# Gate over row sum moved from the attention probabilities to the transposed branch outputs of a hybrid decoder trunk

## The chip, the core and the metric

One core of a Trainium2 chip runs the whole program as one launch. TensorE (PE, with its weight loads as PEld), VectorE (DVE), ScalarE (ACT), GpSimd (POOL) and the queue that starts the DMAs (SP) each take their instructions in a fixed order; semaphores hold an instruction back until its inputs and its output buffer are there. The metric is the device time of the launch in microseconds (us): 1985.64 us before, the median of 3 runs (1984.42 to 1986.34).

## The reference

Two decoder layers on x of 512 tokens by 1024 channels, float32. Each normalises x, projects it, runs three token mixers, merges them by per-channel sigmoid gates, projects back, and ends with a SwiGLU block. The change lies in the mixers A (8 heads in 2 groups, head size 64) and B (8 heads):

```
p_c = masked_softmax(s_c, mask_c);  o_c = einsum(p_c, v_c)      # A: compressed blocks
p   = masked_softmax(s, ...);       o_s = einsum(p, vs)         # A: selected blocks
p_w = masked_softmax(s_w, mask_w);  o_w = einsum(p_w, vw)       # A: window
g   = sigmoid(gate_logits)                                      # per token, head and branch
o   = g[..., 0:1] * o_c + g[..., 1:2] * o_s + g[..., 2:3] * o_w
# B:  o = einsum(masked_softmax(q k), v), no gate
```

With 512 tokens there are 8 blocks and the top 16 of them are taken, and the window is 512 wide, so the selected and the window branch both attend to all earlier tokens, each with its own keys and values.

## The kernel before

Activations lie with channels on the 128 partitions and the 512 tokens along the row, except in the attention, where scores have 128 query tokens on the partitions. Float32 products are made of float32r parts: `split` writes hi = copy (ACT) and lo = source - hi (DVE or POOL), and `mm3` (lines 113 to 115) adds three products. Weights stream from memory, are split the same way (lines 100 and 101, tiles wr, wh, wl) and used by `gemm_gen`.

Attention is a pipeline over 24 jobs in each layer: 16 for mixer A (head h, branch b = 0 selected or 1 window, in the order h0b0, h0b1, h1b0, ...) and 8 for B. `attn` walks steps g; a job starts every 3 steps. In a step:

- `st_s`: score products into a PSUM tile of tag "s" (2 banks); DVE adds the mask and takes the row minimum (line 633); ACT takes the exponential into P0 to P3 and sums the row (line 636).
- `st_n`, at step 4 of the job: for A jobs DVE takes the reciprocal of the row sums (line 643) and multiplies each P by gate and reciprocal (line 645). For B jobs only the reciprocal is taken (line 647), once for a pair of heads.
- `st_t`, TLAG steps behind the scores: PE transposes P into a bank of tag "t" (3 banks, line 660); ACT and DVE split it into the float32r tiles pt or z.
- `st_v`, VLAG steps behind that: value products into the one bank "o" (lines 673 and 674). The two branches of an A head add up in one PSUM group. After the second, ACT and DVE join the hi and lo halves into half of a tile (lines 682, 683); after an odd head PE makes the compressed branch's product (line 688), DVE adds it (689), and the tile is split. For B, ACT spreads the reciprocals over a tile (692), PE transposes it (697), and DVE multiplies (698).

Between these, `fill` lets PE run weight products (the fillers: gates, B's projections, merges) by a rate worked out from due steps, and `step` runs background pieces (rope and norms of later heads, on POOL in this stage). The order within an engine is set when the program is built, by a scheduler that takes ready instructions in program order; weight loads and splits are moved up by 90 places. Tiles of a tag turn through a fixed number of buffers, and a new tile waits until the last reader of the old one is done.

## Time and profile before

| | us |
|---|---|
| median of 3 runs | 1985.64 |
| the profiled execution, its own time | 1982.81 |
| its span, first to last instruction | 1981.0 |
| attention of layer 0, about | 113 to 345 |
| attention of layer 1, about | 1088 to 1322 |

The profile is of one execution. "Busy" is the union of an engine's instructions; matmuls overlap in it, so the distance from one start to the next tells more of PE's pace than a duration. A wait is the idle time in front of an instruction, with the instruction that ended it. [...]

### The profile page before, as it was taken

The numbers are of one execution on the slowest core, as the hardware profiler recorded it, in microseconds if no ns is written. First come the engines' busy times: TensorE is split into PE (matmuls) and PEld (weight loads), VectorE is DVE, ScalarE is ACT, GpSimd is POOL, SyncE is SP. The second block draws the span as 40 slices with busy tenths as digits, with TensorE's granted clock in tenths as the row PEclk, the third lists the DMA queues.
The fourth block names the chain that finished last, engine by engine and source line by source line (L and its number), as shares of the span: only waits on it lengthen the run. The fifth ranks groups of instructions, "written<-read, shape, count | busy, mean of one in ns | idle before, by whom it ended". The sixth has DMA issues, their size and how long they took to land.

```text
span 1981.0 us, 26967 instructions
## 1 busy us (share of the span) xinstructions
PE 1935.6 (98%) x9472; PEld 1627.8 (82%) x9472; DVE 1319.7 (67%) x2783; ACT 996.6 (50%) x1937; POOL 252.0 (13%) x232
## 2 busy tenths in 40 slices
PE   9898999999999999999999899999999999999999
PEld 8777878888888888888888688888888888888887
DVE  8689998788545554455556999878874465534542
ACT  5466776687334332233344577857773343323331
POOL 0453442000000000000004536310000000000000
PEclk9999999999999999999999999999999999999999
DMA  5211101223333223323432111113233322333333
GB/s 159 86 56 34 41 31 43 87 94 104 109 125 101 96 96 93 99 98 96 131 112 93 43 41 44 38 46 100 95 102 119 121 91 100 96 94 99 97 102 100
DMA packets 100519, 173.94 MB, mean 88 GB/s; under 512 B 11936, under 2 KB 26144, under 8 KB 100384
## 3 DMA queue, kind: packets, MB, share of 16 engines
q1 hardware_dynamic: 100384, 172.22, 27.3%
q8 instruction: 74, 1.21, 0.2%
q14 instruction: 61, 0.50, 0.1%
HBM read 167.98 MB, written 4.19 MB: 87 GB/s over the span
## 4 chain that ended last, share of the span: by engine, by line
PE 78%; DVE 8%; ACT 2%; issue 1%; POOL 0%; ACTq 0%; DVEq 0%; POOLq 0%
PE pst L114 9%; PE pst L113 9%; PE pst L115 9%; PE psmm L113 8%; PE psmm L114 8%; PE psmm L115 8%; PE pss L114 7%; PE pss L113 7%; PE pss L115 7%; PE pst L660 1%; DVE P L645 1%; DVE pss L633 1%; PE pso L673 1%; PE pso L674 1%; ACT P L636 1%
## 5 line engine op out<-in xcount | busy, mean ns | idle before, releaser
L100 ACT ACTIVATE wh<-wr 128x512 fp32r<-128x512 f32 (+3 forms) x640 | 387.5, 608 | 698.4 <-PE pst L114 261.0
L101 DVE TENSOR_TENSOR wl<-wr,wh 128x512 fp32r<-128x512 f32 (+2 forms) x526 | 355.1, 676 | 247.5 <-ACT wh L100 242.4
L101 POOL TENSOR_TENSOR wl<-wr,wh 128x512 fp32r<-128x512 f32 (+2 forms) x114 | 138.8, 1224 | 951.8 <-ACT wh L100 935.8
L113 PE MATMUL psmm<-h,wh 128*128 128x512 f32 x600 | 237.2, 395 | 3.7 <-ACT wh L100 2.8
L115 PE MATMUL psmm<-h,wl 128*128 128x512 f32 x600 | 235.2, 392 | 0.6 <-POOL wl L101 0.6
L114 PE MATMUL psmm<-h,wh 128*128 128x512 f32 x600 | 235.0, 392 | 0.0
L113 PE MATMUL pst<-h,wh 128*128 128x512 f32 x512 | 199.8, 390 | 0.0
L114 PE MATMUL pst<-h,wh 128*128 128x512 f32 x512 | 199.3, 389 | 0.0
L115 PE MATMUL pst<-h,wl 128*128 128x512 f32 x512 | 199.3, 389 | 0.0
L113 PEld LDWEIGHTS psmm<-h,wh 128*128 128x128 f32 x600 | 112.9, 188 | 26.4 <-ACT wh L100 3.2
L113 PE MATMUL pss<-h,wh 128*128 128x512 f32 x344 | 134.2, 390 | 0.0
L115 PE MATMUL pss<-h,wl 128*128 128x512 f32 x344 | 133.9, 389 | 0.0
L114 PE MATMUL pss<-h,wh 128*128 128x512 f32 x344 | 133.9, 389 | 0.0
L115 PEld LDWEIGHTS psmm<-h,wl 128*128 128x128 f32 x600 | 112.9, 188 | 24.6 <-POOL wl L101 1.1
L114 PEld LDWEIGHTS psmm<-h,wh 128*128 128x128 f32 x600 | 112.9, 188 | 20.8
L636 ACT ACTIVATE P<-pss,nm 128x512 f32<-128x512 f32 x192 | 100.1, 525 | 55.4 <-DVE nm L633 32.3
L113 PEld LDWEIGHTS pst<-h,wh 128*128 128x128 f32 x512 | 96.1, 188 | 20.2 <-ACT e L984 0.4
L115 PEld LDWEIGHTS pst<-h,wl 128*128 128x128 f32 x512 | 96.1, 188 | 20.1
L114 PEld LDWEIGHTS pst<-h,wh 128*128 128x128 f32 x512 | 96.1, 188 | 19.8
L633 DVE CUSTOM_DVE_ANT_0 pss<-pss,mask 128x512 f32<-128x512 f32 x192 | 93.7, 489 | 7.2 <-PE pss L115 5.8
L660 PE MATMUL pst<-ident,P 128*128 128x128 f32 x480 | 76.6, 274 | 11.5 <-DVE P L645 5.3
L660 PEld LDWEIGHTS pst<-ident,P 128*128 128x128 f32 x480 | 58.2, 141 | 28.1 <-issue 17.8
(423 smaller groups left out, 4303.4 us busy)
## 6 DMA issues: line engine op xcount, KB each, us to landing
wr<-w SPq DMA_DIRECT2D x240, 256.0 KB, 2.6
wr<-wfm SPq DMA_DIRECT2D x188, 256.0 KB, 2.6
wr<-wpc SPq DMA_DIRECT2D x32, 256.0 KB, 2.6
wr<-wo SPq DMA_DIRECT2D x32, 256.0 KB, 2.6
wr<-wb SPq DMA_DIRECT2D x32, 192.0 KB, 2.4
wr<-w SPq DMA_DIRECT2D x32, 192.0 KB, 2.3
mg<-xT SPq DMA_DIRECT2D x16, 256.0 KB, 2.7
wr<-wpa SPq DMA_DIRECT2D x16, 256.0 KB, 2.6
```

Source lines behind the costliest of these rows:

```text
L100: self.A.activation(hi, src, AF.Copy)
L101: (eng or self.V).tensor_tensor(lo, src, hi.bitcast(F32), OP.subtract)
L113: mm(ps, a[0], b[0], start=first, stop=False)
L114: mm(ps, a[0], b[1], start=False, stop=False)
L115: mm(ps, a[1], b[0], start=False, stop=last)
L633: self.V.tensor_tensor_reduce(p[:, :W], p[:, :W], self.mask[:, 512 - W:], 1.0, 3e38, OP.add, OP.min, j.nm[:, i:i + 1])
L636: self.A.activation(j.Pi[i], p[:, :128 * (i + 1)], AF.Exp, bias=j.nm[:, i:i + 1], scale=-1.0, accum_out=j.l[:, i:i + 1])
L645: V.tensor_scalar(j.Pi[i], j.Pi[i], j.gate[:, i:i + 1], j.l[:, i:i + 1], op0=OP.mult, op1=OP.mult)
L660: self.T.transpose(ps[:, c:c + 128], j.Pi[i][:, kt * 128:kt * 128 + 128], self.ident)
L673: T.matmul(o[:, 512 - n:], j.V[kt], h[:, m0:m0 + n], start=j.first and kt == 0, stop=False)
L674: T.matmul(o[:, 512 - n:], j.V[kt], l_[:, m0:m0 + n], start=False, stop=j.last and kt == NT - 1)
```

## The change

The probabilities of mixer A stay unnormalised up to the value products. The sums of a pair of heads are kept per branch (tile lp0 or lp1), inverted and multiplied by the gates as a 128x8 tile, and spread by ACT over a 128x512 tile ("od") right away in `st_n` of the odd head; mixer B does the same without gate. Each branch gets its own group in bank "o", its own transposes of the spread tile (4 on PE) and its own multiplication on DVE; the branches are then added on POOL, and the compressed branch after that on DVE. Transposes go from 6 steps behind the scores to 4, value products from 2 behind them to 3. Tile pt gets 7 buffers, the zero-padded pair z is doubled and alternates by job, results get a tag "od" of 4 instead of "e" (3), and the scratch of software-made DMA descriptors is cut to 1024 bytes.

```diff
-TLAG, VLAG = 6, 2
+TLAG, VLAG = 4, 3
...
-        self.zp = [self.const([128, 512], f"z{j}", F32R) for j in range(2)]
+        self.zp = [[self.const([128, 512], f"z{j}{n}", F32R) for j in range(2)] for n in range(2)]
...
     def st_n(self, j, part):
         V = self.V
-        if j.cmp:
-            a = 2 - 2 * part
-            V.reciprocal(j.l[:, a:a + 2], j.l[:, a:a + 2])
-            for i in (a + 1, a):
-                V.tensor_scalar(j.Pi[i], j.Pi[i], j.gate[:, i:i + 1], j.l[:, i:i + 1], op0=OP.mult, op1=OP.mult)
-        elif j.h % 2 and part:
+        if j.h % 2 and part:
             V.reciprocal(j.lp, j.lp)
+            if j.cmp:
+                V.tensor_tensor(j.lp, j.lp, j.gate, OP.mult)
+            j.lb = self.pg("od")
+            self.A.activation(j.lb.rearrange("p (i h d) -> p i h d", i=NT, h=2),
+                              j.lp.rearrange("p h i -> p i h")[:, :, :, None].to_broadcast([128, NT, 2, 64]),
+                              AF.Copy)
...
     def st_v(self, j, s):
         T = self.T
-        if j.first and s == 0:
+        if s == 0:
             self.o = self.ps("o")
...
-            T.matmul(o[:, 512 - n:], j.V[kt], h[:, m0:m0 + n], start=j.first and kt == 0, stop=False)
-            T.matmul(o[:, 512 - n:], j.V[kt], l_[:, m0:m0 + n], start=False, stop=j.last and kt == NT - 1)
+            T.matmul(o[:, 512 - n:], j.V[kt], h[:, m0:m0 + n], start=kt == 0, stop=False)
+            T.matmul(o[:, 512 - n:], j.V[kt], l_[:, m0:m0 + n], start=False, stop=kt == NT - 1)
         if s < 2:
             return
...
+        odd = j.h % 2
+        if odd:
+            pc = self.ps("t")
+            for i in range(NT):
+                T.transpose(pc[:, i * 128:i * 128 + 128], j.lb[:, i * 128:i * 128 + 128], self.ident)
+        else:
+            self.od[j.b] = self.pg("od")
+        od = self.od[j.b]
+        r, s = (slice(64, 128), slice(0, 64)) if odd else (slice(0, 64), slice(64, 128))
+        self.A.activation(od[r], o[s], AF.Copy)
+        self.V.tensor_tensor(od[r], o[r], od[r], OP.add)
+        if not odd:
+            return
+        self.V.tensor_tensor(od, pc, od, OP.mult)
+        if j.cmp and j.b == 0:
+            return
+        if j.cmp:
+            o0 = self.od[0]
+            self.weng.tensor_tensor(od, od, o0, OP.add)
+            pc = self.ps("t")
+            r = slice((j.h // 2 % 2) * 64, (j.h // 2 % 2) * 64 + 64)
+            T.matmul(pc, self.vbd[j.h // 4][r], self.PcT[r], start=True, stop=True)
+            self.V.tensor_tensor(od, pc, od, OP.add)
...
+        self.split(hi, lo, od, self.weng)
+        self.yo.append((hi, lo))
```

What this does to the order, at three places of layer 0. First DVE where job h1b1 is normalised, before; bbcq and bbckv are the norm of B's compressed inputs, which run at the same time:

```order
L643 RECIPROCAL l_1611<-l_1611 128x2
L153 TENSOR_SCALAR bbckvi_1766<-bbckvv_1762 128x4
L154 TENSOR_SCALAR bbcqy_1743<-bbcqi_1745 128x4
L645 TENSOR_SCALAR P_1609<-P_1609,gth_830,l_1611 128x512
L157 TENSOR_TENSOR bbcqt_1744<-bbcqy_1743 128x4
L154 TENSOR_SCALAR bbckvy_1764<-bbckvi_1766 128x4
L645 TENSOR_SCALAR P_1608<-P_1608,gth_830,l_1611 128x384
L158 SCALAR_TENSOR_TENSOR bbcqt_1744<-bbcqt_1744,bbcqv_1741 128x4
L157 TENSOR_TENSOR bbckvt_1765<-bbckvy_1764 128x4
L643 RECIPROCAL l_1611<-l_1611 128x2
```

In these ten rows only the reciprocals and the products with P belong to the attention. The same place on DVE after (L640 and L642 are the reciprocal and the gate product, L631 the mask and minimum of line 633 before, which stands there as ISA):

```order
L640 RECIPROCAL lp_1379<-lp_1379 128x8
L642 TENSOR_TENSOR lp_1379<-lp_1379,gth_834 128x8
L631 ISA pss_1736,nm_1734<-pss_1736,mask 128x512
L631 ISA nm_1734 128x1
L686 TENSOR_TENSOR od_1706<-pso_1672,od_1706 64x512
L102 TENSOR_TENSOR z_103<-pst_1724,z_102 128x384
L320 TENSOR_SCALAR bbcqv_1747<-pst_1742 128x4
L320 TENSOR_SCALAR bbckvv_1768<-pst_1763 128x4
```

The four products over whole P tiles are gone; two 128x8 instructions stand in their place, and the norm of B comes behind minima and splits of the attention.

Second, PE at the end of the first pair of heads, before (L688 is the compressed branch, L660 the transposes of the next job):

```order
L674 MATMUL pso_1836<-z_103,v_847 128x256
L688 MATMUL pst_1980<-pct_1884,vbd_100 128x512
L660 MATMUL pst_1995<-ident,P_1716 128x128
L660 MATMUL pst_1995<-ident,P_1717 128x128
L660 MATMUL pst_1995<-ident,P_1718 128x128
L748 MATMUL pss_2001<-qk_1203,qk_1279 128x384
```

Here one bank of tag "t" is taken between the last value product and the next transposes. PE at the same place after (L680 transposes the spread tile, L697 is the compressed branch, L659 the transposes of P, L114 to L116 a filler):

```order
L673 MATMUL pso_1919<-z_105,v_851 128x256
L680 MATMUL pst_1958<-ident,od_1786 128x128 x4
L697 MATMUL pst_1967<-pct_1896,vbd_100 128x512
L659 MATMUL pst_1974<-ident,P_1733 128x128
L659 MATMUL pst_1974<-ident,P_1732 128x128
L659 MATMUL pst_1974<-ident,P_1733 128x128
L750 MATMUL pss_1985<-qk_1207,qk_1283 128x512
```

Four transposes have come in, and two banks of tag "t" in a row are taken by the end of the pair where one was.

Third, POOL around the addition of the branches (L694) of the third pair, after; L840 to L846 are the rope of B's queries, L102 the lo half of a split:

```order
L840 TENSOR_TENSOR e_3169<-big_2762,qn_1715 128x8x16
L694 TENSOR_TENSOR od_2793<-od_2793,od_2658 128x512
L844 TENSOR_TENSOR big_2761<-big_2761,qc_1714 128x8x32
L842 TENSOR_TENSOR e_3169<-big_2762,qn_1715 128x8x16
L846 TENSOR_TENSOR big_2761<-big_2761,e_3082 128x8x32
L844 TENSOR_TENSOR big_2762<-big_2762,qc_1714 128x8x32
L846 TENSOR_TENSOR big_2762<-big_2762,e_3169 128x8x32
```

L694 is new on POOL and stands among the rope of two tiles. Beside it DVE at the end of the first pair, after, where L698 adds the compressed branch to what L694 left:

```order
L686 TENSOR_TENSOR od_1706<-pso_1919,od_1706 64x512
L689 TENSOR_TENSOR od_1706<-pst_1958,od_1706 128x512
L631 ISA pss_1985,nm_1984<-pss_1985,mask 128x512
L631 ISA nm_1984 128x1
L698 TENSOR_TENSOR od_1706<-pst_1967,od_1706 128x512
```

One minimum stands between L698 and the product that L694 needs; before, the sum of the compressed branch (line 689) waited for no POOL work.

## Rows read from the trace of the kernel before

**Rows 1.** The page's first part: busy time, share, instructions.

```profile
PE 1935.6 (98%) x9472; PEld 1627.8 (82%) x9472; DVE 1319.7 (67%) x2783; ACT 996.6 (50%) x1937; POOL 252.0 (13%) x232
```

**Rows 2.** Windows over both attention stages and one stretch outside them.

```profile
core 0: us, PE busy (x) PEld busy (x) DVE busy (x) ACT busy (x) POOL busy (x), PEclk, DMA share, GB/s
113.00:150.00 37.00, 31.54 (x165) 24.78 (x163) 36.51 (x107) 20.91 (x52) 22.66 (x17) 1.00 0.16 49
150.00:190.00 40.00, 36.38 (x222) 31.37 (x222) 37.74 (x121) 26.23 (x76) 12.48 (x11) 0.96 0.08 26
190.00:230.00 40.00, 36.93 (x216) 32.09 (x217) 39.32 (x117) 29.34 (x73) 14.31 (x14) 1.00 0.11 32
230.00:270.00 40.00, 35.40 (x211) 29.87 (x210) 39.32 (x119) 29.40 (x78) 24.22 (x28) 1.00 0.17 54
...
345.00:640.00 295.00, 294.61 (x1300) 243.34 (x1299) 196.53 (x306) 166.12 (x256) 1.29 (x1) 1.00 0.32 104
1088.00:1130.00 42.00, 35.27 (x181) 27.30 (x181) 40.42 (x117) 23.81 (x58) 24.29 (x18) 0.99 0.17 55
1130.00:1170.00 40.00, 37.89 (x234) 33.13 (x235) 36.74 (x125) 27.79 (x79) 13.88 (x12) 0.97 0.10 31
1170.00:1220.00 50.00, 49.22 (x297) 44.19 (x296) 47.72 (x156) 40.98 (x104) 22.54 (x22) 1.00 0.14 40
1220.00:1270.00 50.00, 47.98 (x298) 40.37 (x297) 46.25 (x135) 37.70 (x104) 21.80 (x25) 1.00 0.13 41
```

**Rows 3.** Waits of PE, whole run: total us, times, longest us.

```profile
PE pss L748 <- ACT P L636: 10.6, 13, 1.4
PE pst L660 <- DVE P L645: 5.3, 3, 2.7
PE pst L660 <- DVE bbckvt L157: 4.4, 2, 2.9
PE pst L660 <- DVE l L643: 1.9, 1, 1.9
```

**Rows 4.** Groups of DVE, whole run: busy us, mean ns, idle before.

```profile
L645 DVE TENSOR_SCALAR P<-P,gth,l 128x512 f32<-128x512 f32 (+3 forms) x128 | 74.8, 609 | 0.4
...
L683 DVE TENSOR_TENSOR e<-pso,e 64x512 f32<-64x512 f32 x32 | 21.9, 685 | 5.7 <-ACT e L682 5.5
...
L643 DVE RECIPROCAL l<-l 128x2 f32<-128x2 f32 x64 | 9.2, 153 | 0.7 <-ACT P L636 0.7
```

**Rows 5.** Line 645 alone: duration min/median/max in ns, first and last start.

```profile
L645 DVE TENSOR_SCALAR P<-P,gth,l x128: 330/474/2056, 122.7 to 1244.8; 128x512 f32<-128x512 f32 x32, 128x384 f32<-128x384 f32 x32, 128x256 f32<-128x256 f32 x32, 128x128 f32<-128x128 f32 x32
```

**Rows 6.** Timeline of PE at a mixer B pair: start, us, what.

```profile
301.46 0.60 PE L697 MATMUL pst<-ident,e 128*128 128x128 f32 x4
301.90 0.60 PE L544 MATMUL pst<-ident,big 128*96 128x128 f32 x4
```

**Rows 7.** Timeline of PE at the end of a mixer A pair.

```profile
218.32 1.12 PE L688 MATMUL pst<-pct,vbd 64*128 64x512 f32 x2
219.38 0.55 PE L660 MATMUL pst<-ident,P 128*128 128x128 f32 x3
```

**Rows 8.** Timeline of PE behind its longest wait in layer 0's attention.

```profile
162.54 0.63 PE L660 MATMUL pst<-ident,P 128*128 128x128 f32 x4 [2.90 <-DVE bbckvt L157]
...
163.30 0.63 PE L114 MATMUL psmm<-h,wh 128*128 128x512 f32 x1
163.73 0.63 PE L115 MATMUL psmm<-h,wl 128*128 128x512 f32 x1
```

**Rows 9.** A group of ACT: the spread tile of mixer B.

```profile
L692 ACT ACTIVATE e<-lp 128x512 f32<-128x512 f32 x8 | 5.0, 629 | 0.0
```

**Rows 10.** Groups of POOL in layer 0's attention, 113 to 345 us.

```profile
L101 POOL TENSOR_TENSOR wl<-wr,wh 128x512 fp32r<-128x512 f32 x24 | 31.4, 1308 | 66.7 <-ACT wh L100 58.8 <-PE psmm L114 5.2 <-ACT e L576 2.7
...
L101 POOL TENSOR_TENSOR oT<-e,oT 128x512 fp32r<-128x512 f32 x4 | 5.1, 1283 | 9.2 <-ACT oT L100 9.2
```

More of the change, by code (lines that the diff above doesn't have):

```diff
@@ L93, in small @@
     def small(self, shape, tag, dt=F32):
-        return self.sm.tile(shape, dt, tag=tag, name=self.nm(tag), bufs=2 if tag in ("vec", "nm", "l", "lp") else 1)
+        return self.sm.tile(shape, dt, tag=tag, name=self.nm(tag), bufs=2 if tag in ("vec", "nm", "lp0", "lp1") else 1)
     def const(self, shape, name, dt=F32):
@@ L182, in consts @@
         self.vbd = [self.const([128, 128], f"vbd{g}") for g in range(2)]
-        self.zp = [self.const([128, 512], f"z{j}", F32R) for j in range(2)]
-        for t in self.kbd + self.vbd + [z[:, :128].bitcast(F32) for z in self.zp]:
+        self.zp = [[self.const([128, 512], f"z{j}{n}", F32R) for j in range(2)] for n in range(2)]
+        for t in self.kbd + self.vbd + [z[:, :128].bitcast(F32) for p in self.zp for z in p]:
             V.memset(t, 0.0)
@@ L654, in st_t @@
         else:
-            h, l_ = self.zp
+            h, l_ = self.zp[j.n % 2]
         ps = self.ps("t")
@@ L672, in st_v @@
             h, l_, m0, n = j.dst[kt]
-            T.matmul(o[:, 512 - n:], j.V[kt], h[:, m0:m0 + n], start=j.first and kt == 0, stop=False)
-            T.matmul(o[:, 512 - n:], j.V[kt], l_[:, m0:m0 + n], start=False, stop=j.last and kt == NT - 1)
+            T.matmul(o[:, 512 - n:], j.V[kt], h[:, m0:m0 + n], start=kt == 0, stop=False)
+            T.matmul(o[:, 512 - n:], j.V[kt], l_[:, m0:m0 + n], start=False, stop=kt == NT - 1)
         if s < 2:
             return
-        if j.last:
-            odd = j.h % 2
-            if not odd:
-                self.od = self.pg("e")
-            r, s = (slice(64, 128), slice(0, 64)) if odd else (slice(0, 64), slice(64, 128))
-            self.A.activation(self.od[r], o[s], AF.Copy)
-            self.V.tensor_tensor(self.od[r], o[r], self.od[r], OP.add)
-            if odd:
-                if j.cmp:
-                    pc = self.ps("t")
-                    r = slice((j.h // 2 % 2) * 64, (j.h // 2 % 2) * 64 + 64)
-                    T.matmul(pc, self.vbd[j.h // 4][r], self.PcT[r], start=True, stop=True)
-                    self.V.tensor_tensor(self.od, pc, self.od, OP.add)
-                else:
-                    lb = self.pg("e")
-                    self.A.activation(lb.rearrange("p (i h d) -> p i h d", i=NT, h=2),
-                                      j.lp.rearrange("p h i -> p i h")[:, :, :, None].to_broadcast([128, NT, 2, 64]),
-                                      AF.Copy)
-                    pc = self.ps("t")
-                    for i in range(NT):
-                        T.transpose(pc[:, i * 128:i * 128 + 128], lb[:, i * 128:i * 128 + 128], self.ident)
-                    self.V.tensor_tensor(self.od, pc, self.od, OP.mult)
-                if j.cmp:
-                    hi, lo = self.pg("oT", F32R), self.pg("oT", F32R)
-                else:
-                    hi, lo = self.pg("cq", F32R), self.pg("cq", F32R)
-                self.split(hi, lo, self.od, self.weng)
-                self.yo.append((hi, lo))
@@ L706, in attn @@
+        self.split(hi, lo, od, self.weng)
+        self.yo.append((hi, lo))
     def attn(self, jobs, hooks):
         n = 3 * len(jobs)
+        for i, j in enumerate(jobs):
+            j.n = i
         for g in range(n + TLAG + VLAG):
@@ L738, in a_jobs @@
                 j = Job()
-                j.h, j.first, j.last, j.cmp = h, b == 0, b == 1, True
+                j.h, j.b, j.cmp = h, b, True
                 def op(j=j, h=h, b=b):
@@ L918, in b_jobs @@
             j = Job()
-            j.h, j.first, j.last, j.cmp, j.gate = h, True, True, False, None
+            j.h, j.b, j.cmp = h, 0, False
             j.open = lambda: None
```

22 lines of the change are left out of this document (12 added, 10 removed).

## Prediction

> **What bounds the kernel now.** I read the page's first part, then windows, then PE's waits, then the groups of the engine that PE waits for, then PE's timeline. PE is busy for 98% of the span [rows 1], so time can only come from its few idle stretches or from work given to it. The windows say where those are: in 345 to 640 PE idles 0.39 of 295 us, while in the four windows that hold layer 0's mixer A jobs (113 to 270) length less busy time is 5.46 + 3.62 + 3.07 + 4.60 = 16.75 us, and in layer 1's (1088 to 1270) 6.73 + 2.11 + 0.78 + 2.02 = 11.64 us [rows 2]. Together 28.4 of 339 us. In layer 0's windows DVE is busy 36.51 + 37.74 + 39.32 + 39.32 = 152.9 of 157 us, or 97%; ACT 105.9, POOL 73.7 [rows 2]. So this stage has two nearly full engines, and PE waits for DVE: 11.6 us in transposes of P (5.3 + 4.4 + 1.9), and 10.6 us in score products that wait for a bank which ACT has to read, behind DVE's minimum [rows 3]. The 4.4 us have the name of B's norm, yet transposes of P need nothing of that norm; they need line 645, whose instructions stand between the norm's in DVE's order. All 11.6 us are thus waits for the normalisation.
>
> **What is removed.** 128 products over P, 74.8 us, and 64 reciprocals, 9.2 us [rows 4]: 84.0 us of DVE, 42.0 in each layer. These products last 330 to 2056 ns with a median of 474 [rows 5], so some are held up far beyond their length. [...]
>
> **What is added, by engine.**
> PE: 16 groups of four transposes (4 pairs, 2 branches, 2 layers). At a pair of mixer B the same four take 301.90 - 301.46 = 0.44 us from start to start [rows 6]; 16 x 0.44 = **+7.0 us**. Nothing hides this, since PE is the engine that the rest waits for in the end.
> DVE, a layer: 8 more joins of hi and lo at 685 ns, 5.5 us; 8 products from PSUM over 512 columns, taken at the same 685 ns, 5.5 us [rows 4]; 16 instructions of 128x8, bounded by 153 ns [rows 4] and by the 2056 ns of rows 5, taken at 0.2 us, 3.2 us. In all 14.2, so DVE loses 42.0 - 14.2 = 27.8 us a layer, and has 152.9 - 27.8 = 125 us of work left in a stage whose PE work is 140.2 + 3.5 = 143.7 us: 87%.
> ACT, a layer: 8 spread tiles at 629 ns [rows 9] and 8 copies out of "o", taken at as much: 10.1 us, so 116 of 144 us. POOL: 4 additions, as long as a 128x512 split, 1283 ns [rows 10]: 5.1 us. Neither becomes the fullest engine.
> At no cost: the second z pair and the two further pt buffers (memory alone), and the smaller scratch, since all loads are issued from SP. The lag of 4 would put transposes next to exponentials; but the scores of the next job's second step, right behind them in PE's order, wait for the same exponential's bank already, so a wait is brought forward by four transposes, not made. At most 0.44 us at each of the 13 waits of rows 3, 5.7 us; I take 0 and keep 5.7 for the range.
>
> **What PE gets back.** How much idle time is left at a DVE load of 87%? The trace has two windows of the same stage with a load under 97% and all kinds of jobs: 1170 to 1220 (DVE 95%, PE idle 0.78 of 50) and 1220 to 1270 (92%, 2.02 of 50) [rows 2]: 2.8% of the time. On 310.6 + 7.0 us of PE work that is 9.1 us. Line 645 first runs at 122.7 us [rows 5], so what PE waits before cannot change: a quarter of the 37 us window, and of the idle 5.46 and 6.73 us of the two first windows, 3.0 us. Left are 12.1 of 28.4: **-16.3 us**. From the other side: the 11.6 us for normalisation go, and half of the 10.6, which is 16.9. Bounds: 0 (each wait finds another releaser) and -28.4.
> [...] The granted share is 0.96 over 40 us there, and 0.99 over 42 and 0.97 over 40 us in layer 1 behind the wait of 2.7 us [rows 2, 3]: 1.6 + 0.4 + 1.2 = 3.2 us lost. Both waits are waits for line 645, so **-3.2 us**; bounds 0 and -3.2.
>
> **What is late next.** The end of a pair. Its transposes and the compressed product take two "t" banks in a row. The first is free after a copy (0.63), a join and a product (0.685 each), 2.0 us; until PE claims it again there are the compressed product, 219.38 - 218.32 = 1.06 us [rows 7], three transposes, two scores and, in most pairs, six filler matmuls: about 1.06 + 0.33 + 0.45 + 1.36 = 3.2 us, in the third pair 1.8 without the filler. The second bank is free only after the POOL addition (1.28) and line 698 (0.69), 4.0 us, and is wanted about 5 us on. DVE stands still in line 698 until POOL is done; behind it stand the z split, for which value products wait, and minima, for which ACT's exponentials and so the scores wait. On POOL the addition waits for DVE's product, with weight splits for the fillers behind it; on ACT the spread waits for two 128x8 instructions of DVE, with exponentials behind it, one for every second job. So with POOL free there is no wait, and 1 us to spare. POOL is not always free: in the third pair the addition stands amid B's rope. I take 1 us for each of the two third pairs and 0.15 for the other six: **+3.0 us**. Bounds: 0; and, if at each of 8 pairs POOL's row stands behind a weight split that waits 58.8 / 24 = 2.45 us for ACT [rows 10], 1.5 us beyond the spare time, 12 us, with 5 us more for each third pair, 22 us.
>
> **Sum.** +7.0 - 16.3 - 3.2 + 3.0 = -9.5 us. From the profiled execution, 1982.8 us (its span of 1981.0 and 1.8 around it), that gives 1973.3; that execution was 2.8 us under the median of the runs, so the forecast for the median is 1985.6 - 9.5 = **1976 us**.
>
> **Rivals.**
> The waits only move. For it: the chain from score to minimum to exponential stays, with two "s" banks, and the window 1220 to 1270 idles 4% though DVE has 8% of it free [rows 2]. Against: the 11.6 us hang on an instruction that is gone. Half the return: -8.1 - 1.6 + 7.0 + 3.0 = 0.3, **1986 us**, no change.
> The end of the pair becomes the bound: line 698 holds DVE until POOL comes, at every pair. New waits of 22 instead of 3 us make it -9.5 + 19 = +9.5, **1995 us**, slower. It decides from 12.5 us in all, 1.6 us a pair. For it: POOL's idle time is waiting for ACT with the queue shut behind it [rows 10]. Against: the order was made with L694 among instructions that are ready then, and POOL has 83 of 157 us free in layer 0.
> The stage becomes as dense as the rest: 0.1% idle [rows 2] beside the 3.0 us before the first normalisation, so -25.1 - 3.2 + 7.0 = -21.3 and **1964 us**. Against it is that no window of the attention under DVE's full load shows that.
> The transposes lower the clock. Each of the 16 new groups that brought half speed for as long as the long wait did would cost 1.6 us, 26 us in all: **2002 us**. Against: ten transposes of P a job and a granted share of 1.00 in five of the eight windows [rows 2]; it fell behind long waits alone [rows 8]. [...] No row shows a clock that fell among transposes without a wait ahead of it.
> That the change does not do what it says is hardly open: the order shows the removed and the added rows.
>
> **How the numbers follow.** Forecast 0.64, waits only move 0.16, end of the pair 0.10, dense stage 0.08, clock 0.02. The forecast's own range is 1969 to 1983: its return may be 5 us more or less, and the new waits 0 to 8. The range for 8 in 10 reaches to the rivals on both sides, 1965 to 1988: under it lies half of the dense case (0.04), above it the pair end, the clock and the worse end of waits that move (0.14). A change under 0.2% (4 us) cannot be told from none. Under 1981.7: 0.61 of the forecast's 0.64, and 0.08: 0.69. Above 1989.6: 0.10 + 0.02 and 0.02 of the moved waits: 0.14. Between: 0.17.
>
> **What would show it.** Line 660's waits for DVE should fall from 11.6 to under 2 us, the waits of scores for ACT from 10.6 to about 5; DVE busy in the stage's windows near 87%, their PE idle near 12 us in all, the clock 1.00; 96 transposes of spread tiles at 0.11 us apart; the attention stages shorter and 345 to 640 of the same length. Wrong would be: waits of transposes or of line 697 for DVE behind line 698 of 1.6 us or more at most pairs, waits of transposes for ACT, or a granted share under 0.95 in these windows.

## The result and the profile after

The changed kernel is slower: 2001.41 us median (four runs, 1998.42 to 2005.43) against 1985.66 us for the kernel before on the same chip, a ratio of 1.0081 with the interval [1.0062, 1.0101]. That is +15.8 us where -9.5 were forecast, and outside the range of 1965 to 1988 us. The profiled execution took 2002.57 us, 19.8 above the profiled one of before; that is 4 us more than the medians differ by, since the profiled one of before lies 2.8 us under its median and this one 1.2 above its own.

The first part of the page, kernel after, answers to [rows 1]:

```profile
PE 1952.0 (98%) x9536; PEld 1640.3 (82%) x9536; DVE 1289.7 (64%) x2657; ACT 1020.9 (51%) x1971; POOL 257.8 (13%) x240
```

Windows of the kernel before over its two attention stages, from the first score of a layer to its last value product (columns as in [rows 2]; the last of them but two, PEclk, is the granted share of TensorE's clock):

```profile
113.10:344.60 231.50, 213.37 (x1276) 182.45 (x1275) 217.12 (x628) 161.52 (x423) 92.21 (x85) 0.99 0.12 37
1088.70:1322.20 233.50, 221.53 (x1318) 189.72 (x1318) 213.22 (x634) 166.36 (x430) 97.78 (x89) 0.99 0.13 41
```

The same two stages of the kernel after, and six of the shorter windows that answer to [rows 2]:

```profile
113.90:352.10 238.20, 220.90 (x1308) 187.47 (x1307) 195.54 (x564) 172.18 (x439) 96.17 (x89) 0.98 0.11 36
1095.80:1342.30 246.50, 229.47 (x1350) 195.27 (x1350) 201.90 (x570) 176.66 (x446) 101.16 (x93) 0.98 0.12 39
...
113.00:150.00 37.00, 32.05 (x171) 26.06 (x170) 33.35 (x103) 23.11 (x58) 23.77 (x20) 0.96 0.14 45
150.00:190.00 40.00, 38.89 (x238) 33.99 (x238) 30.47 (x105) 28.85 (x79) 10.84 (x9) 0.95 0.10 32
190.00:230.00 40.00, 37.04 (x217) 31.15 (x216) 35.21 (x92) 30.69 (x75) 15.28 (x15) 1.00 0.10 32
230.00:270.00 40.00, 35.51 (x208) 30.24 (x207) 30.53 (x95) 29.77 (x76) 26.45 (x30) 0.96 0.17 53
...
1099.00:1140.00 41.00, 35.98 (x196) 29.54 (x195) 37.25 (x106) 22.02 (x54) 28.16 (x23) 0.96 0.13 43
1140.00:1180.00 40.00, 37.50 (x215) 31.90 (x216) 30.11 (x102) 30.35 (x83) 7.88 (x7) 0.91 0.09 28
```

Nearly all of the 19.8 us lies in the attention: 465.0 us before, 484.7 after, and what is outside them is 1516.0 and 1516.1 us. DVE did get free, 152.9 us before [rows 2] and 129.6 of 157 us now (33.35 + 30.47 + 35.21 + 30.53), 83%. PE did not use it. In the two stages PE idles 484.7 - 450.4 = 34.3 us, against 465.0 - 434.9 = 30.1 before, and it is busy for 15.5 us more, of which the 64 transposes explain 7.0. The granted share fell from 0.99 to 0.98; 0.95 and 0.96 stand in three of layer 0's four windows, where before there was one, and 0.96 and 0.91 in two of layer 1. Length times lost share, as the prediction took it, is 1.5 + 2.0 + 1.6 + 1.6 + 3.6 = 10.3 us in these five windows, against 3.2 before; an estimate, since the shares are rounded. By it about 7 us of the added busy time are work at the lower clock level (0.43 us from one 512-column product to the next in place of 0.23, as the pieces at the end of this document show), more than the 4.2 us of added idle time.

Waits of PE, kernel after (engine, line, what it waited for, total us, times, longest), answer to [rows 3]:

```profile
PE pss L114 <- ACT qk L101: 6.7, 10, 1.4
PE pss L750 <- ACT P L634: 6.1, 8, 1.4
PE pso L672 <- DVE od L686: 5.9, 6, 2.1
PE pst L659 <- ACT pct L615: 4.9, 2, 3.3
```

The 11.6 us behind line 645 are gone and scores wait 6.1 in place of 10.6 us, both as forecast. But the transposes of P (line 659) still wait 10.0 us in all, now for ACT's copy of the compressed probabilities ("pct", 4.9), for line 689 (2.3), for exponentials (2.2) and for B's norm (0.6). Other new waits stand beside them, and their names are those of the change: "od" is a head's output on its way out of the one "o" bank, and "qk" is a tile of mixer B that ACT splits in the step in which it now also copies such an output. Two views show this. First two of the lines that write "od", kernel after (count, duration min/median/max in ns; below, what DVE sat idle for ahead of such lines):

```profile
L686 DVE TENSOR_TENSOR od<-pso,od x48: 673/689/695, 145.6 to 1343.0; 64x512 f32<-64x512 f32 x48
L694 POOL TENSOR_TENSOR od<-od,od x8: 1280/1290/1292, 174.3 to 1275.8; 128x512 f32<-128x512 f32 x8
...
  ACT od L685: 14.0, 16
  POOL od L694: 6.9, 5
```

The durations are those that the prediction took (685 and 1283 ns). What it did not price is that DVE stands still 14.0 us for the copy, against 5.5 before [rows 4]; the 6.9 us that it stands still for POOL were to cost 3.0 with all else at the end of a pair. Then the timeline of ACT and of PE in layer 0's mixer B, kernel after (start us, us, engine, what, and in brackets the idle time before and its releaser):

```profile
296.28 0.59 ACT L685 ACTIVATE od<-pso 64x512 f32<-64x512 f32 x1
296.90 0.59 ACT L101 ACTIVATE qk<-pst 96x512 fp32r<-96x512 f32 x1
...
297.55 0.50 PE L114 MATMUL pss<-qk,qk 96*128 96x512 f32 x1 [1.30 <-ACT qk L101]
```

The copy of a head's output stands right ahead of the qk split in ACT's order, and PE waits 1.30 us for the split.

### The profile page after: what moved, and what is told of

It reads as the page before. It is cut to its first block, busy times and chain, and to the rows that moved or that the text cites. A ratio compares the mean times of both kernels' runs of the same rounds, so it can differ in the third digit from the quotient of the medians.

```text
span 2000.8 us, 26987 instructions
## 1 busy us (share of the span) xinstructions
PE 1952.0 (98%) x9536; PEld 1640.3 (82%) x9536; DVE 1289.7 (64%) x2657; ACT 1020.9 (51%) x1971; POOL 257.8 (13%) x240
## 4 chain that ended last, share of the span: by engine, by line
PE 79%; DVE 11%; ACT 6%; issue 2%; POOL 2%; DMA 0%; SPq 0%; ACTq 0%; DVEq 0%; POOLq 0%
PE pst L115 10%; PE pst L114 10%; PE pst L116 10%; PE psmm L116 8%; PE psmm L114 8%; PE psmm L115 8%; PE pss L114 7%; PE pss L115 7%; PE pss L116 7%; ACT P L634 1%; PE pst L659 1%; DVE pss L631 1%; DVE qk L551 1%; PE pso L672 1%; DVE pt L102 1%
## 5 line engine op out<-in xcount | busy, mean ns | idle before, releaser
L102 DVE TENSOR_TENSOR wl<-wr,wh 128x512 fp32r<-128x512 f32 (+2 forms) x526 | 352.0, 670 | 250.1 <-ACT wh L101 245.3
L102 POOL TENSOR_TENSOR wl<-wr,wh 128x512 fp32r<-128x512 f32 (+2 forms) x114 | 136.9, 1207 | 936.5 <-DVE wl L102 680.9
L114 PE MATMUL psmm<-h,wh 128*128 128x512 f32 x600 | 237.8, 396 | 5.1 <-ACT wh L101 4.4
L116 PE MATMUL psmm<-h,wl 128*128 128x512 f32 x600 | 236.7, 395 | 0.6 <-POOL wl L102 0.6
L114 PE MATMUL pst<-h,wh 128*128 128x512 f32 x512 | 199.6, 390 | 0.0
L116 PE MATMUL pst<-h,wl 128*128 128x512 f32 x512 | 199.2, 389 | 0.0
L114 PEld LDWEIGHTS psmm<-h,wh 128*128 128x128 f32 x600 | 113.9, 190 | 27.5 <-ACT wh L101 4.8
L116 PEld LDWEIGHTS psmm<-h,wl 128*128 128x128 f32 x600 | 113.8, 190 | 25.0 <-POOL wl L102 1.1
L114 PE MATMUL pss<-h,wh 128*128 128x512 f32 x344 | 134.1, 390 | 0.0
L116 PE MATMUL pss<-h,wl 128*128 128x512 f32 x344 | 133.9, 389 | 0.0
L116 PEld LDWEIGHTS pst<-h,wl 128*128 128x128 f32 x512 | 96.1, 188 | 20.1
L115 PEld LDWEIGHTS pst<-h,wh 128*128 128x128 f32 x512 | 96.1, 188 | 19.8
L114 PEld LDWEIGHTS pst<-h,wh 128*128 128x128 f32 x512 | 96.1, 188 | 19.8
L631 DVE CUSTOM_DVE_ANT_0 pss<-pss,mask 128x512 f32<-128x512 f32 x192 | 94.4, 492 | 17.4 <-PE pss L116 11.6
L659 PE MATMUL pst<-ident,P 128*128 128x128 f32 x480 | 78.4, 279 | 10.0 <-ACT pct L615 4.9
L659 PEld LDWEIGHTS pst<-ident,P 128*128 128x128 f32 x480 | 58.8, 143 | 28.3 <-ACT pct L615 5.6
```

Source lines behind the costliest of these rows:

```text
L102: (eng or self.V).tensor_tensor(lo, src, hi.bitcast(F32), OP.subtract)
L114: mm(ps, a[0], b[0], start=first, stop=False)
L115: mm(ps, a[0], b[1], start=False, stop=False)
L116: mm(ps, a[1], b[0], start=False, stop=last)
L631: self.V.tensor_tensor_reduce(p[:, :W], p[:, :W], self.mask[:, 512 - W:], 1.0, 3e38, OP.add, OP.min, j.nm[:, i:i + 1])
L659: self.T.transpose(ps[:, c:c + 128], j.Pi[i][:, kt * 128:kt * 128 + 128], self.ident)
```

## The experiments

Each time is a median beside the kernel before on the same chip (1984.75 to 1986.13 us); "difference" is against that one. Lags are written as transposes behind scores, values behind transposes; "place" is their sum modulo the three steps of a job, that is, in which of them a head ends. The ratio goes by all runs and the difference by medians; e15, where the two disagree in sign, shows no difference.

| run | edit | us | ratio [95%] | difference |
|---|---|---|---|---|
| e1 | after, lags 6, 2 | 1992.62 | 1.0043 [1.0030, 1.0056] | +7.9 |
| e2 | before, lags 4, 3 | 2008.56 | 1.0112 [1.0096, 1.0127] | +23.8 |
| e3 | before, no normalisation | 1967.19 | 0.9914 [0.9902, 0.9927] | -17.6 |
| e4 | after, no spread | 1992.72 | 1.0041 [1.0029, 1.0054] | +8.0 |
| e5 | e3 at lags 4, 3, with the z pairs and pt buffers of after | 1973.42 | 0.9948 [0.9934, 0.9962] | -12.0 |
| e6 | e4 at lags 6, 2 | 1988.42 | 1.0020 [1.0011, 1.0029] | +3.0 |
| e7 | after, lags 5, 2 | 2000.76 | 1.0080 [1.0067, 1.0092] | +15.3 |
| e8 | after, lags 5, 3 | 1987.48 | 1.0011 [1.0003, 1.0020] | +2.0 |
| e9 | after, L694 on DVE | 1994.91 | 1.0059 [1.0046, 1.0072] | +9.5 |
| e10 | e8, L694 on DVE | 1977.52 | 0.9960 [0.9948, 0.9972] | -7.9 |
| e11 | before, 2 of 4 products on ACT | 1981.53 | 0.9981 [0.9973, 0.9990] | -3.9 |
| e12 | before, all products on ACT | 1976.41 | 0.9953 [0.9941, 0.9965] | -9.0 |
| e13 | after, a head's end one step later | 2006.06 | 1.0105 [1.0092, 1.0118] | +20.7 |
| e14 | e10, no spread | 1974.13 | 0.9941 [0.9929, 0.9954] | -11.2 |
| e15 | e10, a head's end behind the scores | 1984.46 | 1.0004 [0.9994, 1.0014] | -0.9 |
| e16 | after, values and end behind the scores | 1994.44 | 1.0040 [1.0026, 1.0053] | +8.3 |
| e17 | e10 at lags 6, 3 | 1998.97 | 1.0067 [1.0054, 1.0080] | +12.8 |

**The four parts of the change, taken apart (e1 to e4).** The theory behind them: relief of DVE pays as forecast, and either the new lags or the new ends of the heads spend it.

```diff
 e1  -TLAG, VLAG = 4, 3          (in after)
     +TLAG, VLAG = 6, 2
 e2  -TLAG, VLAG = 6, 2          (in before; with the z pairs, pt buffers and scratch of after)
     +TLAG, VLAG = 4, 3
 e3  -            V.reciprocal(j.l[:, a:a + 2], ...)        (in before)
     -            for i in (a + 1, a):
     -                V.tensor_scalar(j.Pi[i], ...)
 e4  -        if odd:                                       (in after)
     +        if odd and not j.cmp:      # no transposes of a spread tile for A, no spread on ACT, no product
```

> The changed kernel with the old lags of 6 and 2. Theory 1 (the shorter way from scores to transposes and value products is what costs: waits for the bank of the value products, for the bank behind the compressed branch and for B's queries and keys are of order and latency, not of DVE load): back by 10 us or more, to 1985 to 1992, with the half-rate clock stretches of the attention down from 20.5 us to about 7. Theory 2 (the new form of the pair ends, 64 transposes and a bank per branch, costs by itself): 1997 to 2002 as the changed kernel.

> The kernel before with lags 4 and 3, 7 pt buffers, two z pairs and the small scratch, but the old normalisation of P by DVE. Theory 1 (the lags cost): slower than before by 10 us or more, since line 645 then stands straight in front of the transposes: 1996 to 2010. Theory 2 (the new pair ends cost): within 5 us of 1985.7.

> The kernel before without reciprocal and product over P for mixer A, nothing put in their place (the normalisation and the gates of mixer A are left out). It prices what DVE's relief alone is worth. If PE waits because DVE is full, as the prediction had it: 16 to 20 us less, 1966 to 1970. If the waits are of latency and only find another releaser: 0 to 8 us less, 1978 to 1986.

> The changed kernel without the spread tiles of mixer A, their 64 transposes and the products with them (mixer A stays unnormalised and without the gates of two branches); lags, banks and additions as changed. If the added PE work is the cost: 7 us less and the clock as it is, 1993 to 1995. If the two banks taken in a row at the pair ends, with the waits behind them, cost too: 10 to 15 us less, 1986 to 1991. If the lags cost: no more than 7 us less.

e3 settles the return. Its two stages:

```profile
114.30:337.20 222.90, 212.31 (x1276) 183.68 (x1275) 182.76 (x532) 161.52 (x423) 90.68 (x85) 0.98 0.13 39
1081.30:1306.50 225.20, 219.01 (x1318) 189.31 (x1318) 187.21 (x538) 166.46 (x430) 96.26 (x89) 1.00 0.14 43
```

PE has the same 1276 and 1318 instructions as before and idles 16.8 us in place of 30.1: 13.3 us from idle time, and 17.6 in the medians. So most of the prediction's return (16.3 and 3.2) is there when nothing is added. The clock's part of it is not seen: the share in e3's two stages is 0.98 and 1.00, where it was 0.99 in both. The two lags are then far from free: from e1 to the changed kernel they cost 2001.41 - 1992.62 = 8.8 us, and 23.8 on the old form. That e2 is so much worse has a reason of its own, in the waits of its profiled execution (2000.97 us, the fastest of its five):

```profile
PE pst L660 <- DVE P L645: 17.2, 14, 3.1
```

At a lag of 4 the transposes stand in the step of the normalisation that they need; the new form has no such line, so e2 says little of the change, and e5 was run for it.

**The lags on a relieved DVE, the groups without a spread, and two pairs of lags that tell distance from place (e5 to e8).**

```diff
 e5  e3 with  TLAG, VLAG = 4, 3;   e6  e4 with  TLAG, VLAG = 6, 2
 e7  -TLAG, VLAG = 4, 3          e8  -TLAG, VLAG = 4, 3     (in after)
     +TLAG, VLAG = 5, 2              +TLAG, VLAG = 5, 3
```

> The kernel before without its products over P and their reciprocals (mixer A's branches are neither normalised nor gated), as in the run without normalisation (1967.2 us at lags 6 and 2), but with transposes 4 steps behind scores, value products 3 behind them, two z pairs and 7 pt buffers. Theory that the lags cost by the order in which PE meets its work: 1967 + 9 = 1976 us, as they cost the new form 8.8 us, with PE waits in the A jobs about 8 us longer than without normalisation at the old lags. Rival, that the lags cost only while DVE or the pair ends are late: 1967 to 1970 us.

> The changed kernel without mixer A's spread, its transposes and its product (A's branches are neither normalised nor gated), at lags 6 and 2. What is left against the run without normalisation at the same lags (1967.2 us) is one group of the one o bank, one copy and one join for each branch of a head in place of one for both. Theory that these groups cost by themselves (value products of the next branch wait for the copy and the join): 1992.6 - 8.7 = 1984 us, 17 us above 1967, with waits of value products for the o bank. Rival, that the spread, its transposes and its product hold all of the cost at these lags: 1967 to 1972 us.

> The changed kernel with lags 5 and 2: their sum is 7 as in the changed kernel (4 and 3), so a job's last value products and the pair end stand in the step that opens a new job. Theory that this place costs: 2001 us, as the changed kernel, against 1993 for lags of sum 8. Rival, that the shorter distance from scores to transposes costs: half way, 1997 us, and the same as lags 5 and 3 within 2 us.

> The changed kernel with lags 5 and 3: their sum is 8 as at 6 and 2, so the pair end stands one step behind the one that opens a new job. Theory of the place: 1993 us, as at lags 6 and 2. Rival of the distance from scores to transposes: half way, 1997 us, and the same as lags 5 and 2 within 2 us.

e7 and e8 differ by one step of the value products and by nothing else, and by 13.3 us. Lags 5, 2 with the sum of 7 are as slow as 4, 3; lags 5, 3 with the sum of 8 are 5 us faster than 6, 2. So with the sum at 7 it makes no difference whether transposes stand 4 or 5 steps behind the scores, against the rival, while a step more on either lag alone (e8 beside e7, e8 beside the changed kernel) brings 13 to 14 us: the place of a head's end counts. With the sum at 8 the distance is not free of cost, for 6, 2 is 5 us slower than 5, 3. Waits of PE in e7:

```profile
PE pss L750 <- ACT P L634: 6.4, 9, 1.4
PE pss L114 <- ACT qk L101: 6.1, 11, 1.2
PE pso L672 <- DVE od L686: 5.0, 4, 1.9
```

and in e8:

```profile
PE pss L750 <- ACT P L634: 4.0, 5, 1.4
...
PE pss L114 <- ACT qk L101: 0.8, 1, 0.8
PE pso L672 <- DVE od L686: 0.7, 1, 0.7
```

These three fall from 17.5 to 5.5 us, but others grow, as the sums over the two stages of e7 and of e8 show:

```profile
sum 480.30, PE 449.04 PEld 381.92 DVE 400.46 ACT 349.43 POOL 197.30; mean PE 224.52 PEld 190.96 DVE 200.23 ACT 174.71 POOL 98.65
sum 468.60, PE 441.02 PEld 380.91 DVE 395.28 ACT 349.16 POOL 197.59; mean PE 220.51 PEld 190.45 DVE 197.64 ACT 174.58 POOL 98.80
```

PE idles 31.3 us in e7 and 27.6 in e8, and with the same instructions it is busy for 449.0 and 441.0 us. So two thirds of what the place costs in these profiles is longer busy time, and not the waits themselves. Even without a normalisation the lags cost 1973.4 - 1967.2 = 6 us (e5), less than the 9 expected but not nothing. e6 is 21 us above e3 though it adds neither a spread nor transposes: the rival that the spread holds the cost is out, and what is left are the ends of the heads, one for each branch, and the addition on POOL (with the buffers of the changed kernel).

**The addition on POOL, and a version without a new end (e9 to e12).**

```diff
 e9, e10  -            self.weng.tensor_tensor(od, od, o0, OP.add)
          +            self.V.tensor_tensor(od, od, o0, OP.add)
 e11, e12 +            V.tensor_tensor(j.l[:, a:a + 2], j.l[:, a:a + 2], j.gate[:, a:a + 2], OP.mult)
          -                V.tensor_scalar(j.Pi[i], j.Pi[i], j.gate[:, i:i + 1], j.l[:, i:i + 1], ...)
          +                self.A.activation(j.Pi[i], j.Pi[i], AF.Copy, scale=j.l[:, i:i + 1])   # e11: i odd
```

> The changed kernel with the addition of the two branches (L694) on DVE in place of POOL, lags 4 and 3 as there. Theory of the prediction's second rival (line 698 holds DVE until POOL has come to the addition): in the profile of the changed kernel DVE waited 6.9 us in line 698, five times, so at most 7 us and the clock behind it come back, 1993 us. Rival, that the step in which the pair end stands makes the waits whatever engine adds: 2000 us, no change beyond 2 us.

> The changed kernel at lags 5 and 3 (1987.5 us) with the addition of the two branches on DVE. At these lags the two longest single waits of transposes stand behind line 698 (2.6 and 1.2 us), with half a clock behind them. Theory that POOL's row is what is left there: 3.8 us of waits and up to 4 us of clock, 1980 to 1984 us, faster than the kernel before. Rival, that something else is late as soon as line 698 is not: 1987 us.

> The kernel before, in which two of the four products over P (key lengths 512 and 256, 60% of the columns) go to ACT as a copy with gate over sum as its scale, and the other two stay on DVE with the same one scale; 64 products of 128x2 join on DVE. No pair end and no transposes are added. DVE loses about 0.6 of 74.8 us and gains 64 x 0.15 us, 35 us in all; ACT gains 64 x 0.55 us, so both stand near 85% in the A jobs. Theory that relief of DVE is worth 17.6 us for 84 us taken away, and as much for the part of it that takes DVE under 90%: 1973 us. Rival, that ACT with exponentials for the scores becomes late instead: 1985 us or slower.

> The kernel before with all four products over P on ACT as copies with gate over sum as their scale. DVE loses 74.8 and gains 10 us, ACT gains 128 x 0.5 = 64 us, 32 in each layer, which makes 138 of 157 us or 88% in layer 0. Theory that only DVE's load held PE: 1970 us. Rival, that ACT at 88% holds the exponentials as DVE at 97% held the minima: 1985 us, and slower than with half of the products there.

The addition on POOL costs 2001.4 - 1994.9 = 6.5 us at lags 4, 3 and 1987.5 - 1977.5 = 10.0 at 5, 3. e8 shows how, in layer 1's third pair (DVE, POOL and PE in three pieces of its timeline):

```profile
1235.35 0.69 DVE L698 TENSOR_TENSOR od<-pst,od 128x512 f32<-128x512 f32 x1 [5.62 <-POOL od L694]
...
1233.38 0.72 POOL L846 TENSOR_TENSOR big<-big,e 128x256 f32<-128x256 f32 x1
1234.06 1.26 POOL L694 TENSOR_TENSOR od<-od,od 128x512 f32<-128x512 f32 x1
...
1236.10 1.08 PE L545 MATMUL pst<-ident,big 128*96 128x128 f32 x4 [2.64 <-DVE od L698]
...
1237.40 0.63 PE L115 MATMUL psmm<-h,wh 128*128 128x512 f32 x1
1237.83 0.63 PE L116 MATMUL psmm<-h,wl 128*128 128x512 f32 x1
```

The addition stands behind B's rope on POOL. DVE, which takes its instructions in order, stands in line 698 for 5.62 us with everything behind it, PE waits 2.64 us, and then 512-column products start 0.43 us apart, the lower clock level. That is the prediction's second rival. In e8 DVE waits for POOL at all eight pairs, 12.4 us in all, of which the two third pairs are 4.07 and 5.62. Stages of e10, where this is gone and the head ends at the better place:

```profile
116.20:341.30 225.10, 214.13 (x1308) 186.06 (x1307) 198.34 (x568) 171.68 (x439) 91.48 (x85) 0.99 0.13 39
1085.40:1317.70 232.30, 224.04 (x1350) 193.52 (x1349) 201.72 (x574) 177.13 (x446) 97.17 (x89) 0.99 0.14 41
```

PE has the 1308 and 1350 instructions of the changed kernel, 27.3 us less length, 15.1 us less idle time and 12.2 us less busy time. Against e3's, its busy time is 438.2 - 431.3 = 6.9 us longer, as much as the 64 transposes, priced at 7.0.

e12 takes DVE's products to ACT without new ends of heads and without new banks; its stages:

```profile
115.60:338.90 223.30, 213.55 (x1276) 183.26 (x1275) 194.43 (x596) 187.24 (x487) 91.41 (x85) 0.98 0.13 39
1083.40:1316.00 232.60, 221.88 (x1318) 190.06 (x1317) 195.57 (x602) 192.43 (x494) 96.86 (x89) 0.99 0.14 41
```

DVE is at 87 and 84%, ACT at 84 and 83%, and PE idles 20.5 us. 9 us of 17.6 come back; the theory's 1970 was too good and the rival's 1985 too bad. Half of the products on ACT (e11) brings 5 us less than all of them; the theory had put 3 between the two, and the rival had it the other way round. e10 and e12 are both faster than the kernel before, by 8 and 9 us, and so than the changed one.

**Why the place matters, and what is left (e13 to e17).**

```diff
 e13  +            if q > 0 and q % 3 == 0:        (in after; copy, join, product split off st_v as st_end)
      +                self.st_end(jobs[q // 3 - 1])
 e14  e10 with e4's edit
 e15  e10 with  self.st_end(jobs[q // 3])  behind  self.st_s(j, g % 3)
 e16  after with  self.st_v(jobs[q // 3], 2)  behind  self.st_s(j, g % 3)  and not at the step's start
 e17  e10 with  TLAG, VLAG = 6, 3
```

> The changed kernel at its own lags 4 and 3, its value products where they were; the end of each head (transposes of the spread, copy, join, product, addition on POOL as there, compressed product, split) stands one step later, at the start of the step in which it stands with lags 5 and 3. Theory that the place of the head's end costs (copy and join in the step that opens a job, whose qk tiles and 512-column minimum and exponential wait behind them): 1987.5 us, as at lags 5 and 3. Rival, that the place of the value products costs: 2000 us, as the changed kernel. Between them, 1994, neither holds alone.

> The changed kernel at lags 5 and 3 with the addition on DVE (1977.5 us), without mixer A's spread, its transposes and its product (A's branches are neither normalised nor gated). If the spread costs what the prediction took for its transposes, 7.0 us: 1970.5 us, and one group of the o bank per branch costs 3 us against the run without normalisation (1967.2). Rival, that the groups hold the cost: 1976 us.

> The changed kernel at lags 5 and 3 with the addition on DVE (1977.5 us), in which the end of each head is issued behind the scores of the same step, so that on DVE the join stands behind the minima and need not wait for ACT's copy in front of them. Theory that a join that waits for its copy delays minima and so scores: 1972 us, faster than the kernel before by 13. Rival, that these waits are covered: 1977 us; and if the o bank then comes free too late for the next branch, 1980 us with waits of value products for it.

> The changed kernel at its lags 4 and 3, in which a head's last value products and its end are issued behind the scores of the step in place of at its start. Theory that copy and join cost because they stand in front of the qk splits, the 512-column minimum and its exponential in the step that opens a job: the ten waits of B's scores for ACT's qk (6.7 us) fall under 2 us, and the time is 1990 us. Rival, that what costs is how soon the o bank is claimed again behind the join: the waits of value products for the o bank grow from 5.9 us, and the time is 2005 us.

> The changed kernel at lags 6 and 3 (their sum 9, the third of the three places that a head's end can have among the steps of a job) with the addition on DVE; 1977.5 us at 5 and 3, 1994.9 at 4 and 3. Theory that the step that opens a job is the bad place and the other two are free of it: 1977 to 1980 us. Rival, that the place with one step behind the opening is the only good one: 1990 us.

e14 splits what e10 leaves: 3.3 us for the spread, its transposes and its product, 6.4 us for one group per branch against e3 (which has lags 6, 2 and one z pair). The two stages of e14 as a sum:

```profile
sum 454.20, PE 432.31 PEld 373.11 DVE 392.64 ACT 340.29 POOL 188.27; mean PE 216.15 PEld 186.56 DVE 196.32 ACT 170.14 POOL 94.13
```

PE is busy for 5.9 us less than in e10 but idles 21.9 us in place of 19.2: part of the transposes went into time in which PE would have waited. My 7 and 3 were the wrong way round.

e13 and e15 missed. Both put the join later while the next head claims the one "o" bank as soon as before. Waits of PE in e13, and the sum of its two stages:

```profile
PE pss L114 <- ACT qk L101: 5.2, 10, 1.2
PE pso L672 <- DVE od L687: 5.0, 6, 2.1
...
sum 484.90, PE 447.43 PEld 382.43 DVE 394.42 ACT 347.59 POOL 197.55; mean PE 223.72 PEld 191.21 DVE 197.21 ACT 173.80 POOL 98.77
```

and in e15:

```profile
PE pso L672 <- DVE od L687: 5.3, 2, 4.1
```

In e15 the wait for the bank has grown from 0.7 us in e10 to 5.3; its profiled execution (1989.81 us) lies 5.4 us above its median, so the bank may cost less in the others. In e13 the two stages are 484.9 us long and in the changed kernel 484.7: the move gained nothing there, and the 4 us by which its profiled execution is longer lie outside them, most of it ahead of the first score (117.5 us in place of 113.9); why is open. So neither run shows a gain from moving the end of a head away from its value products, and only e15 shows a cost at the bank. e13 also says that the copy alone is not what holds the qk split: with the copy a step away, its ten waits stay at 5.2 us. e16 moves products and end together, behind the scores of the same step; the waits for the "o" bank and for qk, in e16, and the sum of its two stages:

```profile
PE pss L114 <- ACT qk L101: 4.1, 6, 1.1
...
PE pso L672 <- DVE od L686: 2.7, 5, 1.1
...
sum 476.10, PE 443.61 PEld 378.40 DVE 395.24 ACT 348.35 POOL 197.90; mean PE 221.81 PEld 189.20 DVE 197.62 ACT 174.18 POOL 98.95
```

They fall from 12.6 to 6.8 us, and the time by 7.0, half of what a sum of 8 brings; the rival (a longer wait for the bank) is out, and the theory's 1990 was not reached. Yet PE's idle time falls by 1.8 us only (34.3 to 32.5), since other waits grow; its busy time falls by 6.8, at granted shares of 1.00 and 0.99 in place of 0.98 twice (0.996 in place of 0.994 over the whole profiled execution).

e17, the third place, is 21 us slower than the second. It waits elsewhere, 9.1 us in ten scores for an exponential and 3.8 us for the "o" bank. But e17 does not tell the place from the distance. Its transposes stand 6 steps behind the scores, so a tile of P comes free later, and its exponentials wait for that, a wait of ACT that e10 has once, with 1.1 us:

```profile
ACT P L634 <- PE pst L659: 10.7, 10, 1.7
```

That a sum of 7 is worse than one of 8 is shown; which order of instructions makes it so is not, and what the third place is worth by itself is not either.

## Why the prediction was wrong

The steps between the kernels, each a difference of two runs (each taken against the kernel before on its own chip), in two orders (the terms depend on the order, as POOL's 6.5 or 10.0 shows). The first goes by lags of 5, 3, which neither kernel has:

| step | predicted | measured |
|---|---|---|
| DVE relieved of products and reciprocals | -16.3 - 3.2 | -17.6 (before to e3) |
| one group, copy and join per branch, and lags 5, 3 in place of 6, 2 | in +3.0 | +6.4 (e3 to e14) |
| spread, 64 transposes, product | +7.0 | +3.3 (e14 to e10) |
| addition on POOL | in +3.0 | +9.9 (e10 to e8) |
| lags 4, 3 in place of 5, 3 | 0, at most 5.7 | +13.8 (e8 to after) |
| sum | -9.5 | +15.8 |

The second holds to the lags of the two kernels:

| step | predicted | measured |
|---|---|---|
| DVE relieved of products and reciprocals | -16.3 - 3.2 | -17.6 (before to e3) |
| one group, copy and join per branch, addition on POOL | +3.0 | +20.6 (e3 to e6) |
| spread, 64 transposes, product | +7.0 | +4.9 (e6 to e1) |
| lags 4, 3 in place of 6, 2 | 0, at most 5.7 | +7.9 (e1 to after) |
| sum | -9.5 | +15.8 |

The lengths of the two attention stages in the profiles give the same picture: -16.9, +6.1, +3.2, +11.2 and +16.1 us in the first order, -16.9, +22.3, +4.8 and +9.5 in the second.

1. The return was nearly right: e3 gives 17.6 of 19.5 us, 13.3 of them idle time where 16.3 were forecast, and no wait of transposes for the normalisation is left. e3 takes more from DVE than the change does, since it adds nothing. The clock's 3.2 us, length times lost share behind the waits of 2.9 and 2.7 us of [rows 3], did not come back: no gain of the share is seen in e3, and in the changed kernel the loss grew to about 10.3. That there was a loss, the trace of before shows: from 163.3 to 166.3 us, behind the first of these waits, the granted share is 0.50 and 512-column products start 0.43 us apart, where from 400 to 410 us they start 0.23 us apart.
2. The transposes have about the length that was priced: 6.9 us of PE's busy time between e3 and e10, 5.9 between e14 and e10. "Nothing hides this" does not hold everywhere: with spread and product they cost 3.3 us at lags 5, 3, 4.9 at 6, 2 and 7.8 at 4, 3 (e4 to after).
3. One step that failed is "At no cost". I costed the lags by what a transpose might wait for, and took 0. That reasoning looked at the distance from scores to transposes, which between 5 and 4 steps is worth nothing by itself (e7 beside the changed kernel). I did not look at what the sum of both lags does: it went from 8 to 7 and put every head's end into another step of a job, on ACT, on DVE and before the one "o" bank. From the old lags of 6, 2 it costs 7.9 us, above the 5.7 that I kept, and from 5, 3, the best pair tried, 13.8. The kernel's steps show where the end falls ahead of any run, though not what it costs there.
4. The other step that failed is "What is late next", by as much as the lags in the first order and by more in the second. +3.0 us had a bound of 22 beside it, and the runs give 6.4 + 9.9 = 16.3 in one order and 20.6 in the other, near that bound. I had one mechanism (DVE stands in line 698 until POOL comes, the third pair amid B's rope) and took it at 1 us for each of the two third pairs; e8 shows 5.62 us of DVE and 2.64 of PE at one. The working asked whether POOL is free on average, 83 of 157 us, where the in-order queue at that moment counts. A group, copy and join for each branch was priced on DVE and ACT as load alone, not as something that PE waits for.
5. The rivals. "The end of the pair" was given 0.10, with 1995 us. Its mechanism is there: without the change of lags DVE waits for POOL at every pair (e8), and the addition costs 9.9 us there and 6.5 in the changed kernel. e1, the new form at the old lags, took 1992.62 us. The lags, which are not in this rival, make 2001 of it. "The waits only move" names the profile after (30.1 us of idle time became 34.3) but not its cause: with nothing added, e3 shows that they do not move. "The transposes lower the clock" (2002 us) has the right time for a wrong reason, which is luck: the clock did fall, but e10 has the same 64 transposes and a share of 0.99 in both stages, as the kernel before.
6. DVE's load fell further than the forecast 87%, to 83%, but not through a larger relief: the page's busy time fell by 30.0 us, not by 2 x 27.8, and the longer stage spreads what is left over more time. A group's row counts the whole time of its instructions, also where those of other lines overlap them (in e8 DVE's line 689 starts at 1228.10 us and lasts 0.69, and line 631 behind it starts at 1228.71); the windows count overlapping time once. e3 takes away 84.0 us by [rows 4], and its windows lose 430.35 - 369.98 = 60.4. The long products of line 645 stand beside POOL's work: in the trace of before, 52 of the 128 ran while a POOL instruction ran, and they took up to 2056 ns (867 on average), while none of the other 76 took more than 546 (433 on average). The joins out of PSUM show no such thing: all 48 of line 686 above took 673 to 695 ns, 12 of them beside POOL. What holds the long products up is not shown.

Of the signs, a granted share under 0.95 came in one window (0.91). Waits of transposes for ACT, another sign, came with 4.9 + 2.2 = 7.1 us. The waits of transposes of P for DVE fell to 2.9 us (2.3 + 0.6) where under 2 was forecast. DVE's own waits in line 698 came five times, 6.9 us in eight pairs, where waits of PE behind it of 1.6 us at most pairs had been asked for. PE's idle time in the stage was to be near 12 us in all: it is 37.0 + 3 x 40.0 - 143.5 = 13.5 us in layer 0's windows alone.

## What to carry to other kernels

A lag in a pipeline of steps has a length and a place: before costing a changed lag at nothing, look in which step the end of the work now falls, what each in-order engine has queued there, and whether the one buffer behind it is claimed sooner. An engine that is free for half of a stage is not free for an instruction that another engine waits for in order; cost it by what stands ahead of it in that queue at that moment, and put it on the waiting engine where that is short (here -6.5 and -10.0 us for one changed word of the kernel). A full engine can be relieved by one that does the same work in the same place: e12 gained 9.0 us without a new end, a new bank or a new step. e10, the change with the better place and the addition on DVE, gained 7.9, close to the 9.5 that were forecast for the change as it was.

## What was not expected of the hardware

In this trace the clock does not follow the length of PE's waits. In the kernel after, PE waited 3.31 us at 1230.9 and came back at the full level (512-column products 0.23 us apart), and it waited 0.39 and 0.70 us at 1138.5 and 1139.9, around sixteen one-column products, and came back at the lower one (0.43 us apart). Two pieces of PE's timeline:

```profile
1234.18 0.66 PE L659 MATMUL pst<-ident,P 128*128 128x128 f32 x4 [3.31 <-ACT pct L615]
...
1234.91 0.40 PE L114 MATMUL psmm<-h,wh 128*128 128x512 f32 x1
1235.14 0.39 PE L115 MATMUL psmm<-h,wh 128*128 128x512 f32 x1
```

```profile
1138.86 1.05 PE L318 MATMUL pst<-ones,oT 128*128 128x1 f32 x8 [0.39 <-DVE pt L102]
1140.62 0.69 PE L750 MATMUL pss<-qk,qk 128*128 128x384 f32 x1 [0.70 <-ACT P L634]
...
1141.42 0.63 PE L114 MATMUL psmm<-h,wh 128*128 128x512 f32 x1
1141.85 0.63 PE L115 MATMUL psmm<-h,wh 128*128 128x512 f32 x1
```

The granted share from 1140.3 to 1147 is 0.52, from 1233.5 to 1240 it is 1.00. The prediction's account, "it fell behind long waits alone", does not hold. Whether the waits or the one-column products brought the lower level is not shown.
